# One scan over all 128 partitions for both directions of a state-space layer, the backward half turned round by ScalarE copies, with two sets of scan buffers

## The chip, the cores and the metric

The kernel is one program on one core of a Trainium2 chip. Its time is the device time of one execution in microseconds (us); the median of a few runs is compared. The core has a matrix engine (TensorE, PE in the profile; its weight loads are PEld), a vector engine (VectorE, DVE), a scalar engine (ScalarE, ACT), a general engine (GpSimd, POOL) and the queue that issues transfers (SyncE, SP). Each engine takes its instructions in a fixed order and starts one only when what it waits for is done; whatever stands behind a waiting instruction on that engine waits too.

## The reference

A bidirectional encoder block on x of 1 x 1024 x 1024 in float32. After an RMS norm and a projection, half of the channels go through state-space (S5) scans, the other half through a Fourier mix; then come an output projection and a gated feed-forward part with a short convolution. What the change touches is the scan:

```python
def s5_direction(uf, lam_re, lam_im, log_dt, b_re, b_im, c_re, c_im, reverse):
    ...
    bu = jnp.einsum('gph,blgh->blgp', b_bar, uf)
    a = jnp.broadcast_to(lam_bar, (1, uf.shape[1]) + lam_bar.shape)
    _, states = lax.associative_scan(_ssm_combine, (a, bu), reverse=reverse, axis=1)
    return jnp.einsum('ghp,blgp->blgh', c, states).real

y = s5_direction(..., False) + s5_direction(..., True)
```

There are 32 groups with 64 states each, once forward and once backward in time.

## The kernel before

The 1024 steps are laid as 128 chunks of 8 steps. Within a chunk the work is matrix products; only the state at the chunk borders needs a recurrence, a scan over 128 chunks. The complex factor of the recurrence is split into a modulus (`r8`, the factor of the real scan) and a phase that tables (`wt`) take out before the scan and put back after it.

The 32 groups are 16 batches of two (`NB = 16`, `NG = 2`). On the 128 partitions lie the 64 states of the forward direction (partitions 0 to 63) and the 64 of the backward direction (64 to 127). For each batch `states(b)` does, with the names that the profile shows:

- ACT fills `scr` with the scan's factor `r8`, spread over the chunks (line 740).
- DVE makes two products `r` of the chunk inputs `ps` (in PSUM) and the phase table (line 745); two sums of their halves go into `scd`, real and imaginary part (lines 747 and 749, each on DVE or POOL).
- DVE runs four scans: for the real and for the imaginary part, once partitions 0 to 63 forwards (line 756) and once partitions 64 to 127 read and written backwards (line 757). Two groups lie one behind the other in a row of 260 elements; columns of zeros between them restart the recurrence.
- Two products `x` of the scan's result `so` and the table (line 763) and two sums `yy` (line 764) put the phase back, each on DVE or POOL.

`outputs(b)` multiplies `yy` with the matrices `cm` on PE (tile `py`). Other functions run beside this: `prep` (`b`, `bt`, `bm`, lines 666 to 673), `tables` (`w`, `wt`, lines 710 to 714), `out_matrix` (`c`, `cm`, lines 721 to 725), the Fourier part (`vv`, `cb`, `pq`, `fw`, `yfs`, `yf`, lines 828 to 897) and the lower half of the output projection (`pwo`, `h`, line 931). The string `SEQ` gives the order in which these steps are recorded (`S:3` is `states(3)`), a table `ON` says for some 350 small operations whether DVE or POOL does them, and a scheduler then sets the order on each engine from its own estimate of times. So an edit of one step can move others. `scd`, `scr` and `so` exist once.

After the scans come the gate of the state-space half (line 990 on), the upper half of the output projection and the feed-forward part, where PE works nearly without a pause.

Of the kernel before, what the change touches and what calls it, by code (L numbers as in the profile page):

```python
# [15 lines left out]
AF = mybir.ActivationFunctionType  # L16
ALU = mybir.AluOpType
# [3 lines left out]
P = 128  # L21
# [3 lines left out]
NCH = 128  # L25
# [56 lines left out]
def bc(ap, axis, n):  # L82
    ap = ap.unsqueeze(axis)
    shape = list(ap.shape)
    shape[axis] = n
    return ap.broadcast_to(shape)
# [3 lines left out]
def encoder_block(  # L90
# [8 lines left out]
    V, A, PE, GP = nc.vector, nc.scalar, nc.tensor, nc.gpsimd  # L99
# [9 lines left out]
    def opt(key, default):  # L109
        v = OPT.get(key, default)  # L110
        return {"V": V, "G": GP}.get(v, v) if isinstance(v, str) else v
# [137 lines left out]
    def q(name, shape=(P, G), dt=F32, tag="q", bufs=13):  # L249
        return sp.tile(list(shape), dt, name=name, tag=tag, bufs=bufs)  # L250

    def keep(name, shape=(P, G), dt=F32):
        return sp.tile(list(shape), dt, name=name)

    NG = 2
    NB = G // NG
    W = 130

    xh = big.tile([P, 8, L], F32R, name="xh", tag="x32", bufs=2)
    xl = big.tile([P, 8, L], F32R, name="xl", tag="x32", bufs=2)  # L260
# [11 lines left out]
    def norm1(s):  # L272
        xr = xrs[s]
        ss = const.tile([P, 1], F32, name=f"n1_{s}_ss", tag="ss", bufs=2)
        junk = q(f"n1_{s}_sq", (P, 2 + 2 * NG * W), tag="so", bufs=1).bitcast(BF16)[:, 0:D]
        A.activation(junk, xr, AF.Square, accum_out=ss)
# [58 lines left out]
    r8 = keep("r8")  # L335
# [200 lines left out]
    dmk = keep("dmk", (P, 16))  # L536


    scd = keep("scd", (P, 2, NG, W))
    scr = keep("scr", (P, NG, W))  # L540
    cbr = keep("cbr", (P, 8, 2, 16))
    cbi = keep("cbi", (P, 8, 2, 16))

    def zeros():
        nc.sync.dma_start(dmk[96:128], dmask)
        for t in (scd, scr, cbr, cbi):
            GP.memset(t, 0.0)

    cw = const.tile([P, 188], F32, name="cw")
# [87 lines left out]
    def t2(name):  # L637
        return q(name, (P, 2 * NG * P), tag="t2", bufs=2)
# [97 lines left out]
    def states(b):  # L736

        c = bs[b]
        pst_ = c.ps
        A.activation(scr[:, :, 1:129], bc(r8[:, NG * b:NG * b + NG], 2, NCH), AF.Copy)  # L740
        sv = pst_.rearrange("p (i g c) -> p i g c", i=2, g=NG)
        wv = c.wt.rearrange("p i g j n -> p i g (j n)")
        for i in range(2):
            m = t2(f"r{b}_{i}").rearrange("p (i g c) -> p i g c", i=2, g=NG)
            V.tensor_mul(m, sv, wv if i == 0 else wv[:, ::-1])
            if i == 0:
                opt(f"ra{b}{i}", V).tensor_add(scd[:, 0, :, 1:129], m[:, 0], m[:, 1])
            else:
                opt(f"ra{b}{i}", V).tensor_sub(scd[:, 1, :, 1:129], m[:, 1], m[:, 0])
        n = 2 * NG * W  # L750
        so = q(f"so{b}", (P, 2 + n), tag="so", bufs=1)
        m = NG * W
        rf = scr.rearrange("p g w -> p (g w)")
        for i in range(2):
            df = scd[:, i].rearrange("p g w -> p (g w)")
            V.tensor_tensor_scan(so[0:64, 2 + i * m:2 + i * m + m], rf[0:64], df[0:64], 0.0, ALU.mult, ALU.add)
            V.tensor_tensor_scan(so[64:128, i * m:i * m + m][:, ::-1], rf[64:128, ::-1], df[64:128, ::-1], 0.0,
                                 ALU.mult, ALU.add)
        xs = so[:, 2:2 + n].rearrange("p (i g w) -> p i g w", i=2, g=NG)[:, :, :, :NCH]
        c.yy = q(f"yy{b}", (P, 2, NG, NCH), tag="yy", bufs=2)  # L760
        for i, op in ((0, ALU.subtract), (1, ALU.add)):
            m = t2(f"x{b}_{i}").rearrange("p (i g c) -> p i g c", i=2, g=NG)
            opt(f"xm{b}{i}", V).tensor_mul(m, xs, wv if i == 0 else wv[:, ::-1])
            opt(f"xa{b}{i}", V).tensor_tensor(c.yy[:, i], m[:, 0], m[:, 1], op)
# [176 lines left out]
    def w_out_bottom(n, s):  # L941
        w_out_rows(yf_k, wob[n], s, n)

    acts = {
        "N": norm1, "LW": load_win, "PR": params, "ME": zeros, "LG": load_g, "LX": load_x, "PO": poles, "PW": powers, "IF": input_factor,
        "PH": phasor, "PT": phase_tables, "GS": in_factors, "GO": out_factors, "RB": raw_b, "RC": raw_c,
        "CR": rows, "U": w_in_u, "LU": load_u, "P": prep, "T": tables, "OM": out_matrix, "I": inputs, "S": states,
        "O": outputs, "VI": w_in_v, "F": four_tables,
        "FA": four_fold, "FB": four_rows, "FC": four_cols, "ZS": zsplit, "HL": load_h, "WL": w_out_load,
# [432 lines left out]
    for i in range(2):  # L1382
        w = outer.tile([P, 2, 512], F32R, name=f"du{i}", tag="wp", bufs=NWP).bitcast(F32)
# [69 lines left out]
```

## Time and profile before

| | |
|---|---|
| median of 3 runs | 1065.32 us (1063.32 to 1065.96) |
| profiled execution, its own time | 1065.84 us |
| span in the profile | 1064.1 us |
| busy: PE / DVE / ACT / POOL | 91% / 88% / 44% / 22% |
| scans on DVE | 64, 55.0 us |
| mean granted TensorE clock | 0.972 of full speed |

The batches run from about 100 to 335 us after the span's start. How to read it: "busy" is the time in which an engine executes; the rest it waits, and the profile names what ended most of each wait. A time in a table of stretches is from the span's start. In a timeline the first number is the start, the second the duration, and the square bracket the wait before it.

### The profile page before, as it was taken

The numbers are of one execution on the slowest core, as the hardware profiler recorded it, in microseconds if no ns is written. First come the engines' busy times: TensorE is split into PE (matmuls) and PEld (weight loads), VectorE is DVE, ScalarE is ACT, GpSimd is POOL, SyncE is SP. The second block draws the span as 40 slices with busy tenths as digits, with TensorE's granted clock in tenths as the row PEclk, the third lists the DMA queues.
The fourth block names the chain that finished last, engine by engine and source line by source line (L and its number), as shares of the span: only waits on it lengthen the run. The fifth ranks groups of instructions, "written<-read, shape, count | busy, mean of one in ns | idle before, by whom it ended". The sixth has DMA issues, their size and how long they took to land.

```text
span 1064.1 us, 13493 instructions
## 1 busy us (share of the span) xinstructions
PE 969.6 (91%) x4504; PEld 798.9 (75%) x4504; DVE 939.0 (88%) x1721; ACT 465.5 (44%) x849; POOL 232.0 (22%) x243
## 2 busy tenths in 40 slices
PE   1798878677889999999999999999999999999996
PEld 1677767665767788788888888888887778888874
DVE  6998997999997899999988889888897678999887
ACT  4444222533122656544445444454453455445643
POOL 6247546775653003200000000000000000000400
PEclk9999998878999999999999999999999989999998
DMA  8262002342021323332322322223233399857544
GB/s 242 31 165 65 26 20 91 88 146 79 21 64 58 107 84 114 95 99 95 103 79 72 99 79 85 80 74 99 80 100 108 119 325 387 313 165 238 169 145 158
DMA packets 121595, 126.78 MB, mean 119 GB/s; under 512 B 17921, under 2 KB 86454, under 8 KB 121526
## 3 DMA queue, kind: packets, MB, share of 16 engines
q1 hardware_dynamic: 121382, 125.66, 37.2%
q8 instruction: 35, 0.57, 0.2%
q14 instruction: 34, 0.28, 0.1%
q10 hardware_dynamic: 144, 0.26, 0.1%
HBM read 103.35 MB, written 22.51 MB: 118 GB/s over the span
## 4 chain that ended last, share of the span: by engine, by line
PE 44%; DVE 9%; DMA 3%; issue 2%; ACT 1%; SPq 0%; DVEq 0%; ACTq 0%
PE u L130 33%; PE dqa L130 6%; PE dqb L130 6%; DMA wu<-in_w_up_dram 1%; DVE cg L1106 1%; DVE hb L1327 1%; DVE wo L155 0%; DMA d_3a<-adr 0%; ACT cg L1103 0%; DVE cv L1106 0%; DMA d_8a<-adr 0%; DVE n_t L196 0%; DMA d_7b<-in_w_down_dram 0%; DMA d_9b<-in_w_down_dram 0%; DVE hb L1311 0%
## 5 line engine op out<-in xcount | busy, mean ns | idle before, releaser
L1319 POOL TENSOR_TENSOR hb<-hb,gl 128x512 f32<-128x512 f32 x8 | 13.3, 1690 | 553.0 <-DMA d_9a<-adr 552.8
L130 PE MATMUL u<-xb,wo 128*128 128x512 f32 x528 | 130.0, 390 | 0.2 <-ACT xb L154 0.2
L130 PEld LDWEIGHTS u<-xb,wo 128*128 128x128 f32 x528 | 98.9, 188 | 21.8 <-ACT xb L154 0.6
L130 PE MATMUL u<-xa,wo 128*128 128x512 f32 x408 | 98.8, 390 | 0.6 <-DVE wo L155 0.5
L130 PEld LDWEIGHTS u<-xa,wo 128*128 128x128 f32 x408 | 76.4, 188 | 17.3 <-DVE wo L155 0.9
L154 ACT ACTIVATE wo<-wu 128x512 fp32r<-128x512 f32 x78 | 49.1, 630 | 86.5 <-PE u L130 58.7
L130 PE MATMUL pin<-xh,win 128*128 128x512 f32 x256 | 78.4, 407 | 1.2 <-ACT xh L227 1.2
L1106 DVE SCALAR_TENSOR_TENSOR cg<-ug,cw,cg 128x896 f32<-128x896 f32 (+1 forms) x88 | 62.5, 752 | 13.2 <-ACT cg L1103 13.2
L130 PE MATMUL u<-t4o,wo 128*128 128x512 f32 x264 | 63.4, 389 | 0.0
L1106 DVE SCALAR_TENSOR_TENSOR cv<-uv,cw,cv 128x896 f32<-128x896 f32 (+1 forms) x88 | 62.3, 752 | 0.0
L154 ACT ACTIVATE wo<-ws 128x512 fp32r<-128x512 f32 x32 | 20.2, 631 | 91.0 <-PE u L130 78.4
L130 PE MATMUL pwo<-wo,yf 128*128 128x512 f32 x192 | 49.9, 406 | 8.8 <-DVE h L931 5.3
L130 PEld LDWEIGHTS pin<-xh,win 128*128 128x128 f32 x256 | 49.1, 195 | 11.2 <-ACT xh L227 1.6
L130 PEld LDWEIGHTS u<-t4o,wo 128*128 128x128 f32 x264 | 49.6, 188 | 10.3
L155 DVE TENSOR_TENSOR wo<-wu,wo 128x512 fp32r<-128x512 f32 x78 | 55.1, 706 | 0.0
L130 PE MATMUL u<-t1o,wx 128*128 128x512 f32 x204 | 49.5, 389 | 0.0
L130 PE MATMUL u<-t2o,wx 128*128 128x512 f32 x204 | 49.5, 389 | 0.0
L130 PEld LDWEIGHTS pwo<-wo,yf 128*128 128x128 f32 x192 | 35.2, 192 | 17.4 <-DVE h L931 6.4
L130 PE MATMUL pin<-xl,win 128*128 128x512 f32 x128 | 46.4, 411 | 0.1
L130 PEld LDWEIGHTS u<-t2o,wx 128*128 128x128 f32 x204 | 38.3, 188 | 8.0
L130 PEld LDWEIGHTS u<-t1o,wx 128*128 128x128 f32 x204 | 38.3, 188 | 8.0
L714 ACT ACTIVATE wt<-wt 128x128 f32<-128x128 f32 x32 | 9.9, 309 | 67.8 <-POOL wt L712 44.1
(568 smaller groups left out, 2457.6 us busy)
## 6 DMA issues: line engine op xcount, KB each, us to landing
wu<-in_w_up_dram SPq DMA_DIRECT2D x88, 256.0 KB, 2.9
adr<-cg SPq DMA_DIRECT2D x22, 512.0 KB, 3.0
xr<-in_x_dram SPq DMA_DIRECT2D x8, 512.0 KB, 8.2
win_st<-in_w_in_dram SPq DMA_DIRECT2D x16, 256.0 KB, 2.9
wo_st<-in_w_out_dram SPq DMA_DIRECT2D x16, 256.0 KB, 2.8
h<-in_x_dram SPq DMA_DIRECT2D x8, 512.0 KB, 4.5
hdr<-h SPq DMA_DIRECT2D x8, 512.0 KB, 2.6
hb<-hdr SPq DMA_DIRECT2D x8, 512.0 KB, 6.3
```

The source lines that it names most:

```text
L130: i = PE.matmul(o, lhsT, rhs, start=start, stop=stop, skip_group_check=skip)
L154: A.activation(dst_hi, src, AF.Copy)
L155: return eng.tensor_sub(dst_lo, src, dst_hi.bitcast(F32))
L714: A.activation(wf[:, :, 0:64], wf[:, :, 127:63:-1], AF.Copy, scale=(-1.0 if i else 1.0))
L1106: V.scalar_tensor_tensor(cv[:, lo:hi], src[:, at:at + hi - lo], w, cv[:, lo:hi], ALU.mult, ALU.add)
L1319: GP.tensor_mul(hv(s, n), hv(s, n), gl[:, n * 512:(n + 1) * 512])
L1327: V.tensor_add(hv(s, n), hv(s, n), t)
```

## The change

A batch's chunk inputs for the backward direction are now laid in reversed order, so that one scan over 128 partitions goes forwards for both. The two sums go into a new tile `d` (named `sd`, two buffers). Two ACT copies bring `d` into `scd`: partitions 0 to 63 as they are, 64 to 127 with the chunks reversed (new lines 753 and 754). Then there are two scans instead of four (new line 757), and two more ACT copies bring `so` into a new tile `xs` (named `sx`, two buffers), the upper half reversed again (new lines 760 and 761). `scd` and `scr` now exist twice and are used in turn; a row of two groups is 258 elements instead of 260. Line numbers move by two from `states` on.

```diff
-    W = 130
+    W = 129
...
-    scd = keep("scd", (P, 2, NG, W))
-    scr = keep("scr", (P, NG, W))
+    scds = [keep(f"scd{i}", (P, 2, NG, W)) for i in range(2)]
+    scrs = [keep(f"scr{i}", (P, NG, W)) for i in range(2)]
...
-        for t in (scd, scr, cbr, cbi):
+        for t in (*scds, *scrs, cbr, cbi):
             GP.memset(t, 0.0)
...
-        A.activation(scr[:, :, 1:129], bc(r8[:, NG * b:NG * b + NG], 2, NCH), AF.Copy)
+        scr, scd = scrs[b % 2], scds[b % 2]
+        A.activation(scr[:, :, 1:W], bc(r8[:, NG * b:NG * b + NG], 2, NCH), AF.Copy)
...
+        d = q(f"sd{b}", (P, 2, NG, NCH), tag="sd", bufs=2)
...
-                opt(f"ra{b}{i}", V).tensor_add(scd[:, 0, :, 1:129], m[:, 0], m[:, 1])
+                opt(f"ra{b}{i}", V).tensor_add(d[:, 0], m[:, 0], m[:, 1])
...
+        A.activation(scd[0:64, :, :, 1:W], d[0:64], AF.Copy)
+        A.activation(scd[64:128, :, :, 1:W], d[64:128, :, :, ::-1], AF.Copy)
+        so = q(f"so{b}", (P, 2, NG, W), tag="so", bufs=1)
         for i in range(2):
-            df = scd[:, i].rearrange("p g w -> p (g w)")
-            V.tensor_tensor_scan(so[0:64, 2 + i * m:2 + i * m + m], rf[0:64], df[0:64], 0.0, ALU.mult, ALU.add)
-            V.tensor_tensor_scan(so[64:128, i * m:i * m + m][:, ::-1], rf[64:128, ::-1], df[64:128, ::-1], 0.0,
-                                 ALU.mult, ALU.add)
-        xs = so[:, 2:2 + n].rearrange("p (i g w) -> p i g w", i=2, g=NG)[:, :, :, :NCH]
+            V.tensor_tensor_scan(so[:, i].rearrange("p g w -> p (g w)"), scr.rearrange("p g w -> p (g w)"),
+                                 scd[:, i].rearrange("p g w -> p (g w)"), 0.0, ALU.mult, ALU.add)
+        xs = q(f"sx{b}", (P, 2, NG, NCH), tag="sx", bufs=2)
+        A.activation(xs[0:64], so[0:64, :, :, 0:NCH], AF.Copy)
+        A.activation(xs[64:128], so[64:128, :, :, NCH - 1::-1], AF.Copy)
```

The scheduler makes a new order of it. Where a scan stands it prints SCALAR_TENSOR_TENSOR; numbers behind a name only tell buffers apart. On DVE, batch 3 (the fourth) stood so before:

```order
L745 TENSOR_TENSOR r_0_1331<-ps_1263,wt_1116 128x512
L745 TENSOR_TENSOR r_1_1334<-ps_1263,wt_1116 128x512
L747 TENSOR_TENSOR scd<-r_0_1331 128x2x128
L749 TENSOR_TENSOR scd<-r_1_1334 128x2x128
L756 SCALAR_TENSOR_TENSOR so_1337<-scr,scd 64x260
L757 SCALAR_TENSOR_TENSOR so_1337<-scr,scd 64x260
L756 SCALAR_TENSOR_TENSOR so_1337<-scr,scd 64x260
L757 SCALAR_TENSOR_TENSOR so_1337<-scr,scd 64x260
L763 TENSOR_TENSOR x_0_1343<-so_1337,wt_1116 128x512
L763 TENSOR_TENSOR x_1_1346<-so_1337,wt_1116 128x512
```

and stands so now:

```order
L747 TENSOR_TENSOR r_0_1348<-ps_1275,wt_1124 128x512
L747 TENSOR_TENSOR r_1_1351<-ps_1275,wt_1124 128x512
L749 TENSOR_TENSOR sd_1347<-r_0_1348 128x256
L751 TENSOR_TENSOR sd_1347<-r_1_1351 128x256
L757 SCALAR_TENSOR_TENSOR so_1356<-scr_106,scd_104 128x258 x2
L765 TENSOR_TENSOR x_0_1363<-sx_1359,wt_1124 128x512
L765 TENSOR_TENSOR x_1_1366<-sx_1359,wt_1124 128x512
```

The ACT copies belong between the second `sd` and the scan, and between the scan and the first `x`; on DVE nothing stands at either place. In batch 5 the scheduler put other work there:

```order
L751 TENSOR_TENSOR sd_1735<-r_1_1739 128x256
L694 TENSOR_TENSOR dd_1612<-dd_1612,ds_1615 32x128
L695 TENSOR_TENSOR kf_991<-kf_991,dd_1612 32x128
L757 SCALAR_TENSOR_TENSOR so_1744<-scr_106,scd_104 128x258 x2
L693 TENSOR_TENSOR ds_2098<-ds_2098,dmk 32x128
L723 TENSOR_TENSOR cm_1460<-c_0_1461 128x256
L721 TENSOR_TENSOR c_1_1464<-pst,rawc 128x512
L725 TENSOR_TENSOR cm_1460<-c_1_1464 128x256
L765 TENSOR_TENSOR x_0_1751<-sx_1747,wt_1280 128x512
```

So two instructions stand ahead of the scan there and four behind it. On ACT, in batch 7, the two pairs of copies now stand with this between them:

```order
L753 ACTIVATE scd_104<-sd_1929 64x4x128
L754 ACTIVATE scd_104<-sd_1929 64x4x128
L814 ACTIVATE fw<-ft_1965 128x512
L814 ACTIVATE fw<-ft_1968 128x512
L780 ACTIVATE ys_1825<-py_1920 128x2x8x16
L673 ACTIVATE bm_1906<-pbm_1907 128x512
L814 ACTIVATE fw<-ft_1971 128x512
L680 ACTIVATE kf_1692<-pk_1913 128x32
L681 ACTIVATE kb_1693<-pk_1913 128x32
L760 ACTIVATE sx_1941<-so_1938 64x512
L761 ACTIVATE sx_1941<-so_1938 64x512
L741 ACTIVATE scr_106<-r_97 128x2x128
```

Before, the same seven instructions stood on ACT without copies around them. The fill of `scr` now follows the copies out of `so`.

## Rows read from the trace of the kernel before

**Rows 1.** Busy time of the engines in stretches of the span (us of each engine with the number of instructions, then the granted TensorE clock, the DMA share and GB/s): the stage of the scans as a whole, ten microseconds of it, its end, and a stretch after it.

```profile
100.00:330.00 230.00, 184.30 (x1005) 154.16 (x1004) 215.59 (x348) 69.22 (x188) 147.35 (x164) 0.90 0.21 62
...
310.00:320.00 10.00, 10.00 (x54) 8.59 (x53) 9.91 (x17) 1.20 (x4) 3.70 (x4) 1.00 0.28 83
...
300.00:345.00 45.00, 41.81 (x204) 34.14 (x203) 38.41 (x54) 12.72 (x27) 20.08 (x18) 0.96 0.19 55
...
500.00:600.00 100.00, 100.00 (x443) 82.57 (x442) 89.52 (x136) 46.43 (x65) 0.00 (x0) 1.00 0.29 90
```

**Rows 2.** Waits in that stage (who waits for whom: us in total, times, longest): of DVE the longest and the last of its eleven rows, with those on POOL, and the longest of all engines.

```profile
DVE bt L667 <- PE pk L130: 2.2, 1, 2.2
...
DVE r L745 <- POOL yy L764: 1.2, 2, 0.6
DVE cm L725 <- POOL c L721: 1.1, 1, 1.1
DVE w L710 <- POOL wt L712: 1.1, 1, 1.1
DVE cb L839 <- POOL vv L834: 1.0, 1, 1.0
DVE bt L667 <- POOL b L666: 1.0, 1, 1.0
...
DVE cb L844 <- POOL vv L835: 0.2, 1, 0.2
ACT scr L740 <- DVE so L757: 56.8, 14, 8.0
```

**Rows 3.** Groups of DVE instructions in the stage (busy us, mean ns of one, idle before them).

```profile
L756 DVE TENSOR_TENSOR_SCAN so<-scr,scd 64x260 f32<-64x260 f32 x32 | 28.0, 875 | 0.2
L757 DVE TENSOR_TENSOR_SCAN so<-scr,scd 64x260 f32<-64x260 f32 x32 | 27.0, 844 | 0.5
L745 DVE TENSOR_TENSOR r<-ps,wt 128x512 f32<-128x512 f32 x32 | 21.0, 679 | 1.4 <-POOL yy L764 1.2
L666 DVE TENSOR_TENSOR b<-gst,rawb 128x512 f32<-128x512 f32 x19 | 20.8, 1117 | 0.7 <-POOL yy L764 0.6
L763 DVE TENSOR_TENSOR x<-so,wt 128x512 f32<-128x512 f32 x22 | 19.3, 906 | 0.3
L667 DVE TENSOR_TENSOR bt<-b 128x256 f32<-128x256 f32 x22 | 15.8, 740 | 3.4 <-PE pk L130 2.2 <-POOL b L666 1.0
```

**Rows 4.** The first line of the scans alone: shortest, median and longest of its 32 instructions in ns, first and last start.

```profile
L756 DVE TENSOR_TENSOR_SCAN so<-scr,scd x32: 678/692/1591, 109.0 to 326.7; 64x260 f32<-64x260 f32 x32
```

**Rows 5.** Timeline of DVE: two instructions of the same kind, on 128 and on 32 partitions, and batch 3 from its second sum to the first product of the next batch.

```profile
101.97 0.29 DVE L712 TENSOR_TENSOR wt<-w 128x128 f32<-128x128 f32 x1
...
110.17 0.29 DVE L695 TENSOR_TENSOR kf<-kf,dd 32x128 f32<-32x128 f32 x1
...
140.00 0.41 DVE L749 TENSOR_TENSOR scd<-r 128x256 f32<-128x256 f32 x1
140.33 0.68 DVE L756 TENSOR_TENSOR_SCAN so<-scr,scd 64x260 f32<-64x260 f32 x1
...
142.45 0.70 DVE L757 TENSOR_TENSOR_SCAN so<-scr,scd 64x260 f32<-64x260 f32 x1
143.18 1.29 DVE L763 TENSOR_TENSOR x<-so,wt 128x512 f32<-128x512 f32 x2
```

**Rows 6.** Timeline of ACT: a fill of `scr` behind that scan, two copies of 512 elements in a row, and a copy that DVE waits for; the last line is the DVE instruction that it releases.

```profile
143.24 0.42 ACT L740 ACTIVATE scr<-r 128x256 f32<-128x256 f32 x1 [3.76 <-DVE so L757]
...
216.85 1.15 ACT L154 ACTIVATE yf<-yfs 128x512 fp32r<-128x512 f32 x2 [0.18 <-DVE yfs L893]
...
345.08 0.63 ACT L154 ACTIVATE wot<-wo_st 128x512 fp32r<-128x512 f32 x1 [2.37 <-DMA wo_st<-in_w_out_dram]
...
345.75 0.69 DVE L155 TENSOR_TENSOR wot<-wo_st,wot 128x512 fp32r<-128x512 f32 x1 [1.65 <-ACT wot L154]
```

**Rows 7.** Timeline of DVE: one each of the small instructions that the new order puts beside the scans.

```profile
179.21 0.41 DVE L725 TENSOR_TENSOR cm<-c 128x256 f32<-128x256 f32 x1
...
194.07 0.68 DVE L155 TENSOR_TENSOR fw<-pq,fw 128x512 fp32r<-128x512 f32 x1
...
277.33 0.69 DVE L931 TENSOR_TENSOR h<-h,pwo 128x512 f32<-128x512 f32 x1
```

**Rows 8.** Timeline of ACT around batch 7: three of the seven instructions that now stand between the pairs of copies.

```profile
195.68 0.38 ACT L778 ACTIVATE ys<-py 128x256 f32<-128x256 f32 x1 [1.01 <-PE py L130]
196.10 0.60 ACT L673 ACTIVATE bm<-pbm 128x512 f32<-128x512 f32 x1
196.60 0.62 ACT L812 ACTIVATE fw<-ft 128x512 fp32r<-128x512 f32 x1
```

**Rows 9.** The clearing of the scan buffers on POOL (line 547): shortest, median, longest in ns, first and last start.

```profile
L547 POOL MEMSET scd<- x1: 534/534/534, 1.0 to 1.0; 128x520 f32 x1
L547 POOL MEMSET scr<- x1: 314/314/314, 1.8 to 1.8; 128x260 f32 x1
```

More of the change, by code (lines that the diff above doesn't have):

```diff
@@ L746, in states @@
             if i == 0:
-                opt(f"ra{b}{i}", V).tensor_add(scd[:, 0, :, 1:129], m[:, 0], m[:, 1])
+                opt(f"ra{b}{i}", V).tensor_add(d[:, 0], m[:, 0], m[:, 1])
             else:
[L749 to L753, printed above, removed]
-        for i in range(2):
-            df = scd[:, i].rearrange("p g w -> p (g w)")
-            V.tensor_tensor_scan(so[0:64, 2 + i * m:2 + i * m + m], rf[0:64], df[0:64], 0.0, ALU.mult, ALU.add)
-            V.tensor_tensor_scan(so[64:128, i * m:i * m + m][:, ::-1], rf[64:128, ::-1], df[64:128, ::-1], 0.0,
-                                 ALU.mult, ALU.add)
-        xs = so[:, 2:2 + n].rearrange("p (i g w) -> p i g w", i=2, g=NG)[:, :, :, :NCH]
+                opt(f"ra{b}{i}", V).tensor_sub(d[:, 1], m[:, 1], m[:, 0])
+        A.activation(scd[0:64, :, :, 1:W], d[0:64], AF.Copy)
+        A.activation(scd[64:128, :, :, 1:W], d[64:128, :, :, ::-1], AF.Copy)
+        so = q(f"so{b}", (P, 2, NG, W), tag="so", bufs=1)
+        for i in range(2):
+            V.tensor_tensor_scan(so[:, i].rearrange("p g w -> p (g w)"), scr.rearrange("p g w -> p (g w)"),
[3 more added lines that the diff above has]
+        A.activation(xs[64:128], so[64:128, :, :, NCH - 1::-1], AF.Copy)
         c.yy = q(f"yy{b}", (P, 2, NG, NCH), tag="yy", bufs=2)
```

## The prediction

> **What bounds the kernel now.** First the busy times by stretch. While the batches run, from 100 to 330 us, DVE is busy 215.6 of 230 us, ACT 69.2 and POOL 147.4; PE reaches 184.3, at 0.90 of its full clock [rows 1]. DVE carries this stage. At its end PE takes over: it is busy in all of the ten microseconds from 310 on, and then for 100 of 100 us from 500 on [rows 1]. So what DVE gains or loses before about 306 us moves the end by as much; what the last three batches gain behind that is covered by PE. Next the waits: DVE has eleven, 11.6 us in all, the longest 2.2 us; eight of them, 6.8 us, are on POOL. The longest wait of the whole stage is ACT's for the scans, 56.8 us, and nothing on the path hangs on it [rows 2]. Then the groups: the 64 scans cost 28.0 + 27.0 = 55.0 us, a quarter of DVE's stage [rows 3].
>
> **What the change removes.** 64 scans over 64 partitions become 32 over 128, each 258 long instead of 260. Does a scan over twice the partitions take longer? No row has one. A two-input operation of 128 elements takes 0.29 us on 32 partitions and 0.29 on 128 [rows 5], so I take the same time. One scan costs 860 ns on average, though its median is 692 and its longest 1591 [rows 3, 4]. The products `r`, with one input in PSUM, never stretch: 679 ns for 512 elements, while `x` of the same size with both inputs in SBUF takes 906 and `b` 1117 [rows 3]. Something holds up what reads SBUF twice, and POOL is the engine that works beside it. At the mean the saving is 32 x 0.860 = 27.5 us; if only the undisturbed time goes it is 32 x 0.692 = 22.1; if a scan took twice as long it would be nothing. I take 27.5, since a scan that isn't there can't be held up, and keep 22.1 for the rivals.
>
> **What it adds.** Four copies of 512 elements per batch on ACT, 64 in all. The nearest rows are ACT copies of 512 elements on 128 partitions: two in a row take 1.15 us [rows 6]. 32 pairs are 36.8 us of ACT's time, which lifts it from 69 to 106 of 230 us; there is room. Bounds for a pair: 2 x 0.42 by the copy of 256 elements and 2 x 0.63 by two that don't overlap [rows 6]. The price lies in the order. A DVE instruction that used the result of the one ahead of it now waits for ACT. From DVE to ACT: the last scan ends at 142.45 + 0.70 = 143.15, ACT starts at 143.24, so 0.09. From ACT to DVE: 345.08 + 0.63 = 345.71, DVE starts at 345.75, so 0.04 [rows 5, 6]. One hand-over is 0.09 + 1.15 + 0.04 = 1.28 us, two per batch. All 32 uncovered would be 41.0 us, more than the saving. Behind the waiting scan stands everything else on DVE, and POOL and PE wait for that.
>
> How many are covered? I went through the new order batch by batch and set the DVE instructions between sum and scan, and between scan and `x`, against 1.28 us, at their short durations of 0.41 for `cm` and 0.68 for `fw` or `h` [rows 7]. Batch 3 has nothing at either place, as the order in the section on the change shows: 2.56 us of standing, against 3.4 saved at the mean and 1.4 at the median. Batch 5 covers both almost wholly. Ahead of the scans, batches 0 to 15 leave 1.3, 1.0, 0.9, 1.3, 0.9, 0.1, 1.3, 1.3, 0, 1.3, 0.9, 0, 0.9, 0.6, 0, 0.6, together 12.4 us. Behind them they leave 0.6, 1.3, 0.9, 1.3, 1.3, 0, 1.3, 1.3, 0, 1.3, 0, 1.3, 1.3, 0, 0 and 1.3, together 13.2, and I add 0.9 for POOL's `x` in batch 13. That is 26.5 us, as if 20.7 of the 32 were bare.
>
> Four smaller terms. ACT takes its instructions in order: in batch 7 seven of them now stand between the two pairs of copies, some 2.5 us from start to start (0.4 to 0.5 each for the larger ones [rows 8]), while the two scans take 1.4, so 1.1 more; batch 0 gives 0.6. With as much again for places that I didn't see, +3 us. In return DVE's busy share falls from 94% to 82%. The stretching of scans, `x`, `b` and `bt` beyond their short times (0.69, 0.68, 0.68, 0.41) is about 31 us in the rows, 26 of it left when half the scans are gone, and falls by about an eighth: -3.3 us. While DVE stands, POOL catches up on part of the 6.8 us: -2. Batches 13 to 15 save 5.2 and stand 2.5, and this 2.7 stays under PE: +2.7.
>
> At nothing I put the rest. ACT no longer waits with the fill of `scr` alone, but the copies out of `so` wait for the same scan, so little behind it starts earlier. Two more buffers are cleared on POOL: 0.53 + 0.31 us in the first three microseconds [rows 9], long before the first scan. If that cover went it would be 0.85.
>
> Sum against the profiled execution's own 1065.84 us: -27.5 + 26.5 + 3 - 3.3 - 2 + 2.7 = -0.6, so 1065.2. That execution lies 0.5 above the median of the runs, which gives 1064.7.
>
> The Trainium skill speaks against the copies. "ScalarE: Activation LUTs", section "Rules for kernel authors", budgets about 0.3 us for an ACTIVATE and 0.83 ns for each element. An estimate by that page is 0.72 us for a copy and 1.45 for a pair, 0.3 more at each of 20.7 bare hand-overs, so 6 us more and 1071. The pair of 1.15 us that was measured decides [rows 6].
>
> **The rivals.** *Better covered.* ACT is idle most of the time, so its queue may cost nothing (-3); DVE standing still may end all of POOL's waits (-4.8 more) and halve the stretching again (-3.3): 11 us less, 1053. For it speaks that DVE's waits on POOL are short ones; against it that these relieve only where POOL is behind at that moment.
>
> *Slower: ACT's queue.* The mechanism is one: a copy stands behind one more ACT instruction that isn't done. An ACT instruction takes 69.2 / 188 = 0.37 us on average [rows 1]; at 20.7 bare hand-overs that is 7.7 us, so 1072. It decides as soon as more than 27.5 / 1.28 = 21.5 hand-overs' worth of waiting is bare, and I count 20.7. Batch 7 speaks for it; ACT's low share against it.
>
> *Slower: the hold-ups are passed on.* If POOL holds whatever DVE instruction comes, a scan that is gone hands its hold-up to the next. Then only 22.1 us are saved, 5.4 less: 1070. For it speaks that scans with a median of 692 reach 1591. Against it, DVE stands still more often and POOL passes in those gaps. The Trainium skill's page "SBUF — State Buffer", section "Who interferes with whom", says that a DVE instruction with two SBUF inputs and a GpSimd instruction that reads SBUF contend and that one blocks; `r` at 679 ns with no stretching agrees.
>
> *It doesn't do what it says*, a scan over 128 partitions taking twice as long: 1092. The rows of 0.29 us speak against it; I give it nothing of its own.
>
> **How the numbers follow.** What a measurement of this kernel can tell from no change is about 0.3%, 3.2 us. The forecast, that gain and standing cancel, 1064.7, has 0.40 and its own range is 1060 to 1069; 0.09 of it lies faster, 0.27 within the bound and 0.04 slower. Better covered has 0.31, ACT's queue 0.21, the passed-on hold-ups 0.08. So faster 0.09 + 0.31 = 0.40, same 0.27, slower 0.04 + 0.21 + 0.08 = 0.33. The range reaches past the rival on either side, 1050 to 1078; all hand-overs bare (14.5 us more than now, 1079) or all covered (1038) stay outside.
>
> **What will show it.** 32 scans at 0.69 to 0.9 us each; pairs of copies at 1.15; DVE waiting on ACT for `scd` and `sx` about 26 us in all, near 2.5 in batch 3 and near none in batch 5; DVE busy about 30 us less over the stage, and the gate of the state-space half starting within 4 us of where it did. I am wrong if DVE's waits for those copies come to under 18 or over 35 us, if the other two-input operations keep their mean times, or if PE's granted clock in the stage moves by more than a few hundredths of its 0.90.

## The result and the profile after

The changed kernel takes 1067.82 us (median of nine runs, 1066.13 to 1069.73), the kernel before in the same session 1064.51 (1062.23 to 1066.75). The ratio is 1.0031, with a 95% interval of 1.0018 to 1.0044: slower by 3.3 us, between 1.9 and 4.7. The forecast was 1064.7 us, "that gain and standing cancel". The time lies inside the forecast's range. "Slower" by more than 0.3% had a chance of 0.33; the measured 0.31% sits on that bound, and its interval excludes only that nothing changed.

The profiled execution of the changed kernel lies low among its nine: its own time is 1066.17 us, its span 1064.4, against 1065.84 and 1064.1 before, where it lies high. So the two traces explain 0.3 us of the 3.3 directly; they show what the operations cost, and the ratios of repeated runs show what that is worth.

Busy time by stretch in the changed kernel, with the columns of [rows 1]:

```profile
100.00:330.00 230.00, 179.19 (x1002) 151.88 (x1001) 182.13 (x313) 107.76 (x248) 145.38 (x163) 0.89 0.21 62
...
500.00:600.00 100.00, 100.00 (x442) 82.61 (x441) 89.46 (x137) 46.52 (x65) 0.00 (x0) 1.00 0.28 88
```

The prediction expects DVE busy about 30 us less; it is 33.5 less (215.59 in [rows 1]) and ACT 38.5 more. PE's clock is 0.89 instead of 0.90. From 500 to 600 us nothing has changed. The same stretch reaches 230 us all the same, so DVE now stands for 33.5 us more. Whom it waits for, from 100 us to the start of the gate of the state-space half at 347.2 us (who waits for whom: us in total, times, longest):

```profile
DVE x L765 <- ACT sx L761: 14.6, 12, 2.5
DVE so L757 <- ACT scd L754: 10.8, 10, 1.4
DVE sg L993 <- issue: 4.2, 1, 4.2
DVE bt L667 <- POOL cm L725: 3.5, 1, 3.5
DVE yy L766 <- POOL x L765: 3.4, 2, 2.2
DVE cm L725 <- POOL c L721: 2.7, 2, 1.7
DVE r L747 <- ACT wt L714: 2.6, 1, 2.6
DVE b L666 <- POOL yy L766: 1.9, 1, 1.9
DVE r L747 <- POOL yy L766: 1.7, 3, 0.6
...
DVE w L710 <- POOL wt L712: 1.0, 1, 1.0
...
DVE a L847 <- POOL vv L837: 0.8, 1, 0.8
...
DVE c L721 <- POOL cm L723: 0.6, 1, 0.6
...
```

The first two rows are the hand-overs: 25.4 us at 22 of 32 places, 10.8 ahead of the scans and 14.6 behind them. Among the rows under them is what the prediction missed: DVE's waits on POOL, eight rows, are 15.6 us by these names; before they were 6.8 [rows 2]. One of the eight is PE's. `bt` doesn't read `cm`; it exists once, PE's `pk` of the batch before reads it, and it starts 0.10 us after the last of these ends (167.69 + 0.39 = 168.08):

```profile
167.69 0.39 PE L130 MATMUL pk<-cbi,bt 128*128 128x32 f32 x2
...
168.18 0.99 DVE L667 TENSOR_TENSOR bt<-b 128x256 f32<-128x256 f32 x1 [3.55 <-POOL cm L725]
```

It waited for `pk` before too (2.2 us). Without it DVE's waits on POOL are 12.1 us.

The groups that answer to [rows 3] (busy us, mean ns of one, idle before them):

```profile
L757 DVE TENSOR_TENSOR_SCAN so<-scr,scd 128x258 f32<-128x258 f32 x32 | 24.9, 818 | 10.8 <-ACT scd L754 10.8
L747 DVE TENSOR_TENSOR r<-ps,wt 128x512 f32<-128x512 f32 x32 | 21.3, 682 | 4.7 <-ACT wt L714 2.6 <-POOL yy L766 1.7
L666 DVE TENSOR_TENSOR b<-gst,rawb 128x512 f32<-128x512 f32 x19 | 19.1, 1023 | 2.0 <-POOL yy L766 1.9
L765 DVE TENSOR_TENSOR x<-sx,wt 128x512 f32<-128x512 f32 x22 | 15.0, 711 | 14.6 <-ACT sx L761 14.6
L667 DVE TENSOR_TENSOR bt<-b 128x256 f32<-128x256 f32 x22 | 13.5, 631 | 3.5 <-POOL cm L725 3.5
```

A scan over 128 partitions takes what one over 64 took. 55.0 us of scans have become 24.9, and `x`, `b` and `bt` are held up less. Batch 3 on DVE, as in [rows 5]:

```profile
140.90 0.41 DVE L751 TENSOR_TENSOR sd<-r 128x256 f32<-128x256 f32 x1
142.66 1.28 DVE L757 TENSOR_TENSOR_SCAN so<-scr,scd 128x258 f32<-128x258 f32 x2 [1.35 <-ACT scd L754]
145.28 1.29 DVE L765 TENSOR_TENSOR x<-sx,wt 128x512 f32<-128x512 f32 x2 [1.33 <-ACT sx L761]
147.19 0.69 DVE L747 TENSOR_TENSOR r<-ps,wt 128x512 f32<-128x512 f32 x1 [0.62 <-POOL yy L766]
```

and on ACT:

```profile
141.35 0.63 ACT L753 ACTIVATE scd<-sd 64x512 f32<-64x512 f32 x1 [2.60 <-DVE sd L751]
142.00 0.63 ACT L754 ACTIVATE scd<-sd 64x512 f32<-64x512 f32 x1
143.98 0.63 ACT L760 ACTIVATE sx<-so 64x512 f32<-64x512 f32 x1 [1.35 <-DVE so L757]
144.62 0.63 ACT L761 ACTIVATE sx<-so 64x512 f32<-64x512 f32 x1
```

Both hand-overs are bare here, 1.35 and 1.33 us. The two copies of a pair don't overlap: 141.35 to 142.63 is 1.28 us, about the upper of the prediction's two bounds (2 x 0.63), not the 1.15 that it took from [rows 6]. The next batch's `r` starts at 147.19, where it started at 145.09 before. In batch 7 the wait behind the scans is 2.48 us, as the prediction feared, with seven instructions on ACT between the pairs:

```profile
202.03 0.69 DVE L765 TENSOR_TENSOR x<-sx,wt 128x512 f32<-128x512 f32 x1 [2.48 <-ACT sx L761]
```

### The profile page after: what moved, and what is told of

It reads as the page before. It is cut to its first block, busy times and chain, and to the rows that moved or that the text cites. A ratio compares the mean times of both kernels' runs of the same rounds, so it can differ in the third digit from the quotient of the medians.

```text
span 1064.4 us, 13516 instructions
## 1 busy us (share of the span) xinstructions
PE 965.3 (91%) x4504; PEld 796.5 (75%) x4504; DVE 906.1 (85%) x1689; ACT 505.0 (47%) x913; POOL 231.1 (22%) x245
## 4 chain that ended last, share of the span: by engine, by line
PE 50%; DVE 5%; DMA 2%; issue 1%; ACT 1%; DVEq 0%; ACTq 0%
PE u L130 34%; PE dqa L130 9%; PE dqb L130 7%; DMA wu<-in_w_up_dram 1%; DVE cg L1108 1%; DVE wo L155 0%; DMA d_7b<-in_w_down_dram 0%; DVE n_t L196 0%; ACT cg L1105 0%; DMA first_st<-in_w_down_dram 0%; DVE hb L1313 0%; DMA d_9b<-in_w_down_dram 0%; DMA d_5b<-in_w_down_dram 0%; DMA d_3b<-in_w_down_dram 0%; DVE n_y L197 0%
## 5 line engine op out<-in xcount | busy, mean ns | idle before, releaser
L130 PEld LDWEIGHTS u<-xa,wo 128*128 128x128 f32 x408 | 76.4, 188 | 17.6 <-DVE wo L155 1.1
L221 PE MATMUL n_pt<-ident,xr 128*128 128x128 f32 x64 | 13.2, 358 | 26.3 <-DVE xr L292 9.6
```

Source lines behind the costliest of these rows:

```text
L130: i = PE.matmul(o, lhsT, rhs, start=start, stop=stop, skip_group_check=skip)
L221: PE.transpose(pt[:, k * P:(k + 1) * P], xk, ident)
```

## The experiments

The theories, as the expectations name them. *Hand-over*: DVE pays for standing between two of its own instructions while ACT copies, and for what comes of it. *Order*: the scheduler has made a new order, and its waits are that order's, whatever runs in it. *PE*: PE limits the stage, so DVE's gain is hidden anyway. A percentage below is the ratio to the kernel before in the same session; 1% is 10.65 us.

### Buffers, and the copies one place at a time

The first four kernels were left to the scheduler. The kernel before with two sets of buffers:

```diff
-    scd = keep("scd", (P, 2, NG, W))
+    scds = [keep(f"scd{i}", (P, 2, NG, W)) for i in range(2)]
...
+        scr, scd = scrs[b % 2], scds[b % 2]
```

> The kernel before with scd and scr twofold and nothing else: still four scans per batch, no copies. If the slowdown comes from the hand-overs to ACT and what follows from them, the buffers alone are worth nothing: 1064 to 1066 us, and DVE's waits in the batches stay near 12 us. If it comes from the new order that the scheduler makes as soon as anything in the stage changes, this kernel too moves by 2 us or more, with DVE's waits on POOL grown as in the changed kernel.

Measured: 1063.55 us, ratio 1.0001 (0.9988 to 1.0014). The buffers are worth nothing, and by themselves they move nothing.

The changed kernel without copies, and with those at one of the two places:

```diff
-        d = q(f"sd{b}", (P, 2, NG, NCH), tag="sd", bufs=2)
+        d = scd[:, :, :, 1:W]
...
-        A.activation(scd[0:64, :, :, 1:W], d[0:64], AF.Copy)
-        A.activation(scd[64:128, :, :, 1:W], d[64:128, :, :, ::-1], AF.Copy)
...
-        A.activation(xs[0:64], so[0:64, :, :, 0:NCH], AF.Copy)
-        A.activation(xs[64:128], so[64:128, :, :, NCH - 1::-1], AF.Copy)
+        xs = so[:, :, :, 0:NCH]
```

> The changed kernel without any ACT copy: the sums go straight into scd and x reads so, so 32 scans of 128 partitions remain. It leaves out the turning round of the backward half. Theory hand-over: DVE loses 33.5 us of busy time and the 25.4 us of waits for copies don't come, and with them the other waits (23 us in the changed kernel) fall back to about 12, as before; the gate starts some 30 us earlier, 1036 us. Rival order: the other waits stay near 23 us because they belong to the new order, 1046 us. Rival PE: what DVE gains is mostly hidden because PE becomes the bound of the stage, 1055 us or more.

> The changed kernel with the copies ahead of the scan alone; x reads so directly. It leaves out the second turning, so the upper half of the result is in the wrong order. Theory hand-over: 10.8 us of waits for these copies and half of the 11 us of other waits, 16 us over the kernel without copies: 1052 us. Rival order: the waits for scd cost their 10.8 us alone, and the other waits are what the order gives, near 23 us: 1057 us. Rival PE: no more than 3 us from the kernel without copies.

> The changed kernel with the copies behind the scan alone; the sums go straight into scd. It leaves out the first turning. Theory hand-over: 14.6 us of waits for sx and half of the 11 us of other waits, 20 us over the kernel without copies: 1056 us, and the excess of this one and of the one with the copies ahead add up to that of the changed kernel over the kernel without copies. Rival order: 14.6 us alone, other waits near 23: 1060 us, and the two don't add up. Rival PE: no more than 3 us from the kernel without copies.

Measured: 1058.44 us without copies (0.9953, 0.9936 to 0.9970), 1050.43 with those ahead of the scan (0.9890, 0.9872 to 0.9908), 1056.01 with those behind it (0.9948, 0.9930 to 0.9966). The first was expected at 1036 us by *hand-over*, 1046 by *order* and 1055 or more by *PE*, so by itself it would speak for *PE*. But the kernel without any copy is the slowest of the three, so nothing adds up. Each has its own order, and what the orders differ by hides the copies. No theory is told apart by kernels that the scheduler arranges anew.

### The order held

So the order was made a quantity of its own. From the finished order of one kernel, a list per engine says which instruction follows which; each is made to follow the one before it in another kernel too:

```diff
+        for a, b in zip(names, names[1:]):
+            tc.add_manual_dep(
+                here["I-" + b], "I-" + a,
+                mybir.DependencyInfo(mybir.DependencyClass.NoSync, mybir.DependencyReason.DATA),
+                reason="issue order",
+            )
```

Of DVE, POOL, ACT and PE all instructions are held, from the input matrices of the first batch to the sums or outputs of the last. Copies that the order's own kernel doesn't have, or has otherwise, find their place freely.

> The changed kernel, with the instructions of DVE, POOL, ACT and PE between the first batch's tables and the last batch's sums held in the order that the kernel before has; the four copies of a batch go where the scheduler finds room. In that order hardly anything stands between sum, scan and x, so more hand-overs are bare: 28 to 32 of them at 1.28 us, 36 to 41 us of waits for copies, against 33.5 us of DVE time saved. Theory order: the other waits of DVE fall from 23 us to the 12 us of the kernel before, so 1065 to 1072 us. Theory hand-over: they stay at 20 us or more, because POOL and PE are late with what comes from a DVE that stands, 1075 us or more.

> The kernel before with twofold buffers, four scans and no copies, with the instructions of the four engines held in the order of the changed kernel. Theory order: the 11 us of other waits came with that order, so this kernel shows them too, about 23 us in all, and takes 1070 us or more. Theory hand-over: the order costs nothing by itself, DVE's waits stay near 12 us and the time at 1063 to 1066 us.

> One scan over 128 partitions and no copies, in the order of the kernel before: the scan saving alone. It leaves out the turning round of the backward half. Theory order: the 33 us of DVE time come off the stage nearly in full, because no other order spoils them: 1033 to 1042 us, where the same kernel in the scheduler's own order took 1058. Rival PE: TensorE with its lower clock becomes what DVE and POOL wait for, and no more than 10 us come off: 1053 us or more.

> One scan over 128 partitions and no copies, in the order of the changed kernel; it leaves out the turning round of the backward half. With it each of the three sets of operations has run in that order or can be set against it: four scans took 1066, one scan with copies 1068. In the order of the kernel before, the copies cost 32 us (1078 against 1047). Theory hand-over (the 25 us of waits for copies are paid in full): 1043 us. Rival cover (of what DVE gains, only about half reaches the end, as 33 us became 18 in the order of before, so the copies in the order that was made for them cost half of their waits): 1053 to 1057 us. Theory order (the order is bad for whatever runs in it): 1060 us or more.

Measured, with the runs of the kernels before and after in the table:

| | order of before | order of after |
|---|---|---|
| four scans, no copies | 1.0000 | 1.0011 (1.0000 to 1.0021) |
| one scan, no copies | 0.9832 (0.9817 to 0.9847) | 0.9850 (0.9830 to 0.9870) |
| one scan, four copies | 1.0127 (1.0107 to 1.0148) | 1.0031 (1.0018 to 1.0044) |

This takes the 3.3 us apart. The new order alone costs 0.11%, 1.2 us (0 to 2.2). In it the scans save 1.61%, 17 us. In it the copies cost 1.81%, 19 us; by the intervals either is known to some 2 us. What is left of two large terms is 2 us, and the order's 1.2 comes on top. The trace doesn't locate the 1.2: with four scans in the new order the gate starts at 346.0 us, 1.0 earlier than before. In the order of before the scans save 1.68% and the copies cost 2.95%, 31 us: the new order is the scheduler's work to cover them. There DVE waits 36.0 us for copies:

```profile
DVE so L757 <- ACT scd L754: 20.8, 15, 2.9
DVE x L765 <- ACT sx L761: 15.2, 11, 2.1
```

The same two rows of the changed kernel, above, are 10.6 us less, most of it ahead of the scans.

Without copies, in the order of after, the stretch up to the gate is this (busy times as in [rows 1]):

```profile
100.00:324.70 224.70, 190.15 (x1086) 163.28 (x1085) 195.13 (x327) 76.81 (x198) 149.41 (x165) 0.92 0.23 69
```

and with them:

```profile
100.00:347.20 247.20, 195.85 (x1083) 165.47 (x1082) 192.09 (x327) 116.24 (x262) 149.22 (x166) 0.90 0.21 63
```

DVE is idle for 224.70 - 195.13 = 29.6 us in the one and 55.1 in the other. The difference, 25.5, is as much as the 25.4 us of waits for copies; DVE's busy time is 3.0 less with the copies, and the gate starts 22.5 us later. So *hand-over* holds in kind, but not in full: it gave 1043 us without copies in the order of after, *cover* 1053 to 1057, and 1049.62 came. In the order of before 1046.63 came, between the 1033 to 1042 of *order* and the 1053 of *PE*. With the copies there, 1078.38 is in *hand-over*'s range (1075 or more), while DVE's other waits ahead of the gate, 17.6 us, lie between what either theory gave. *PE* falls as the limit: PE gave way by 22 us as soon as DVE didn't stand. Of *order* its first half is right and its second wrong. Four scans in the new order do show DVE's waits ahead of the gate's grown, from 14.3 to 20.0 us:

```profile
DVE bt L667 <- PE pk L130: 3.3, 1, 3.3
DVE cm L725 <- POOL c L721: 2.7, 2, 1.7
DVE r L746 <- ACT wt L714: 2.6, 1, 2.6
DVE b L666 <- POOL yy L765: 1.8, 1, 1.8
DVE r L746 <- POOL yy L765: 1.7, 3, 0.6
...
```

but 1070 us or more were expected and 1066.3 came: DVE is also held up less in that order, and its busy time up to the gate is 7.0 us less than before. (*Hand-over* gave 1063 to 1066, with waits near 12.) The product `x` there, with four scans and no copies:

```profile
L764 DVE TENSOR_TENSOR x<-so,wt 128x512 f32<-128x512 f32 x22 | 14.8, 700 | 0.3
```

It took 906 ns in [rows 3]. With one scan and no copies, in the same order, it is back:

```profile
L761 DVE TENSOR_TENSOR x<-so,wt 128x512 f32<-128x512 f32 x22 | 19.2, 899 | 0.3
```

So neither a standing DVE nor ACT's copies are needed for 700 ns. What runs on POOL beside it matters: in the traces of before, of after, and of the order of after without copies with four scans and with one, 134 scans and `x` on DVE have no POOL instruction beside them, and none of them takes over 699 ns; of the 146 that have one, 79 take over 760. Running beside POOL isn't enough, though, and which POOL instructions do it wasn't separated.

All four copies in the order of the kernel that has only those ahead of the scan:

> The changed kernel with all its copies, in the order of the kernel that has the copies ahead of the scan alone (the fastest so far, 1050 us). Theory order: of the 14 us between that one and the changed kernel a part is the order, the second pair of copies adds at most 16 bare hand-overs of 1.28 us, 20 us; since that order leaves room for few of them, 1060 to 1070 us. Theory hand-over: the pair behind the scan costs its waits of 15 us and as much again in waits elsewhere, 1072 us or more.

Measured: 1079.63 us, 1.0139 (1.0124 to 1.0154). The time is in *hand-over*'s range (1072 or more). Of 31.1 us of waits for copies 18.7 are behind the scan, where the kernel of that order has none, and DVE's other idle time up to the gate grew by 10 us, not by as much again as expected.

### How long a copy may take

With the order of after held, one copy over 128 partitions at each place, which turns nothing:

```diff
-        A.activation(scd[0:64, :, :, 1:W], d[0:64], AF.Copy)
-        A.activation(scd[64:128, :, :, 1:W], d[64:128, :, :, ::-1], AF.Copy)
+        A.activation(scd[:, :, :, 1:W], d, AF.Copy)
```

> The changed kernel, in its own order on every engine, with one ACT copy over 128 partitions at each of the two places instead of two over 64; it leaves out the turning round of the backward half. A hand-over is then 0.09 + 0.63 + 0.04 = 0.76 us instead of 1.28. Theory hand-over (what is paid is the standing time): of 25.4 us of waits for copies some 10 to 11 go; taking both pairs away brought 18 us for 25, so these bring 7 to 8: 1060 us. Rival crossing (what is paid is that DVE has to go through ACT's queue at all, whatever the copy takes): 2 us or less, 1066 us or more.

Measured: 1055.55 us, 0.9914 (0.9892 to 0.9936). Its waits for copies:

```profile
DVE x L763 <- ACT sx L759: 7.5, 10, 1.9
DVE so L756 <- ACT scd L753: 4.5, 7, 0.8
```

12.0 us instead of 25.4, and the time is 1.17% less, 12.5 us, where *hand-over* expected 7 to 8. So the time follows the waits, by about 0.9 us for each of these; taking away the other 12.0 brought another 0.64%, 7 us, 0.6 for each. The rival, that the crossing as such costs (1066 us or more), falls.

Then a version that leaves nothing out: the copies split by real and imaginary part, so that the first two run beside the second sum or scan.

```diff
+            A.activation(scd[0:64, i, :, 1:W], d[0:64, i], AF.Copy)
+            A.activation(scd[64:128, i, :, 1:W], d[64:128, i, :, ::-1], AF.Copy)
```

> The changed kernel with each pair of copies of 512 elements split into two pairs of 256, one for the real and one for the imaginary part: the first pair can run while the second sum (or the second scan) does. Theory hand-over: the wait ahead of x falls from 1.28 to about 0.8 us and the wait ahead of the first scan to about 0.6, so of 25 us of waits some 12 go, and half of that reaches the end: 1062 us. Rival ACT queue: 64 more instructions on ACT, 14 us more, and four places instead of two where a copy can stand behind other work: 1068 us or more.

> The copies split by real and imaginary part, as in the kernel that took 1063.7 us, with the other instructions in the order of the changed kernel. Theory hand-over: the shorter wait is what helped, so it helps here too: waits for copies near 18 us instead of 25, 1062 to 1064 us. Rival order: the 4 us came from another order, and here the time stays at 1067 us or more.

Measured: 1063.68 us in its own order (0.9981, 0.9966 to 0.9996) and 1063.04 in the order of after (0.9985, 0.9968 to 1.0001). The second is in *hand-over*'s range (1062 to 1064), the first 2 us above its 1062. With the order held that is 0.46% less than the changed kernel, 5 us, for 17.4 us of waits for copies instead of 25.4. Part of the 8 us came back: DVE's waits on ACT apart from these copies went from 6.1 to 11.0 us, with 64 more instructions in ACT's queue.

### Other ways to turn the backward half

Each sum in two halves of 64 partitions, the upper one written in reversed order, without copies:

```diff
+            for hs, to in ((LO, scd[LO, i, :, 1:W]), (HI, scd[HI, i, :, NCH:0:-1])):
```

> The same result as the changed kernel without its ACT copies: each sum is made in two halves of 64 partitions, the upper one written in reversed chunk order. 39 more sums of 0.34 us from start to start on DVE, 13 us, against 33 us less for scans and stretching, and no hand-over; 25 more of about 0.5 us on POOL. DVE's balance is 20 us. Theory hand-over: without waits for ACT the balance counts, and as 33 us became 18 at the end, 20 become 11: 1053 us. Rival order: the scheduler's own order spoils it as it did for the kernel without copies (1058 where the order of before gave 1047): 1063 us or more.

Measured: 1074.07 us, 1.0085 (1.0068 to 1.0102), slower than both and a miss. Up to the gate DVE is busy 228.5 us, where without copies, in the order of after, it is 195.1. Of these 33.4 us the sums take 27.9 (52.9 for 78 against 25.0 for 39), 0.72 for each one more and not 0.34; the rest lies in other instructions of another order. A sum over 64 partitions isn't cheaper, and it reads SBUF twice:

```profile
L752 DVE TENSOR_TENSOR scd<-r 64x256 f32<-64x256 f32 x26 | 15.5, 594 | 0.3
```

The inputs turned by PE, which reads the chunks backwards for the upper 64 columns of weights:

```diff
+                for hs, st in ((LO, 1), (HI, -1)):
+                    c.s_last = PE.matmul(pst_[hs, n * P:(n + 1) * P], c.bm[:, i, g, hs],
+                                         cts[ct].u[:, NG * sb + g, ::st], start=True, stop=True)
```

> The same result with the inputs turned by PE: per batch eight products with 64 columns of weights in place of four with 128, the upper four reading the chunks in reversed order; the table of phases for the upper half takes the other sign, and only the sums yy are made in halves. DVE's balance is 33 - 17 x 0.34 = 27 us; PE gets 64 products of 0.3 us more, 19 us. Theory hand-over: DVE decides, half of 27 us reaches the end: 1050 us. Rival PE: the stage is as much PE's as DVE's, and 19 us of PE's time eat the gain: 1062 us or more.

> The kernel whose inputs PE turns (1058.8 us in the scheduler's own order), with the instructions of the four engines in the order of the kernel before. The kernel without copies took 1047 in that order and 1058 in its own. Theory order: this one gains as much, less what 17 more sums on DVE cost: 1050 to 1054 us. Rival PE: 64 more products on PE are the limit in any order: 1058 us or more.

> The same kernel in the order of the changed kernel, where the one without copies took 1050 us. Theory order: 1052 to 1056 us. Rival PE: 1058 us or more.

Measured: 1058.81 us in its own order (0.9944, 0.9926 to 0.9962), 1067.35 in that of before (1.0023, 1.0009 to 1.0037), 1060.26 in that of after (0.9960, 0.9946 to 0.9975). Faster than both kernels, but no more than half of what was expected, and in the order of before not at all. By the times alone the rival *PE* (1058 us or more, 1062 in the kernel's own order) would have it in both held orders. The traces speak against it. The sixteen half products of a batch run in pairs, two starting some 10 ns apart, and take no longer than the eight whole ones did, so the 19 us of PE's time that the expectation counted didn't come. Before, and with the halves (from the last but one kernel of this section, which turns the inputs in the same way):

```profile
105.29 1.14 PE L733 MATMUL ps<-u,bm 128*128 128x128 f32 x8
...
137.96 1.09 PE L734 MATMUL ps<-u,bm 128*64 128x128 f32 x16
```

What costs is on DVE. The 34 halved sums `yy` take 25 to 27 us, 786 ns on average in the kernel's own order, where 17 whole ones took 13.4. DVE is busy 216.3 us up to the gate in the order of before and 208.0 in that of after, and the gate starts 8.1 us later; the sums differ by 1.1 us of it, the scans by 3.5 and `b` by 3.2. Why they are held up more in one order isn't settled.

Last, the copies moved to where no DVE instruction waits for them: PE turns the inputs, and the sums `yy` are turned by ACT on their way to PE.

```diff
+            opt(f"xa{b}{i}", V).tensor_tensor(yy[:, i], m[:, 0], m[:, 1], op)
+            A.activation(c.yy[0:64, i], yy[0:64, i], AF.Copy)
+            A.activation(c.yy[64:128, i], yy[64:128, i, :, ::-1], AF.Copy)
```

> The same result with no copy between two instructions of DVE: PE turns the inputs, and the upper half is turned back by ACT copies of the sums yy, which go on to PE alone. No half sums, so DVE does what it does in the kernels without copies (1047 to 1058 us in three orders); PE has 64 products more, and its last products of a batch start some 1 us later. Theory hand-over: a copy costs where DVE waits for it, so this one costs next to nothing, 1048 to 1056 us. Rival PE: 1058 us or more.

Measured: 1055.83 us, 0.9902 (0.9882 to 0.9921): 10 us faster than the kernel before, 14 faster than the change, the fastest of those that leave nothing out, and at the upper end of what *hand-over* gave (1048 to 1056). ACT copies for 26 us here:

```profile
L765 ACT ACTIVATE yz<-yy 64x256 f32<-64x256 f32 x32 | 13.2, 415 | 25.7 <-DVE yy L764 18.6 <-POOL yy L764 4.1 <-DVE cb L846 2.9
L766 ACT ACTIVATE yz<-yy 64x256 f32<-64x256 f32 x32 | 13.1, 413 | 0.4
```

and none of DVE's waits up to the gate is for one of these copies, in a list that begins

```profile
DVE h L933 <- PE pwo L130: 7.6, 5, 2.0
DVE cm L723 <- POOL c L721: 5.5, 1, 5.5
DVE wot L155 <- ACT wot L154: 3.8, 1, 3.8
...
```

What the copies cost here beyond DVE's waits isn't separated: this kernel has its own order, and without copies 1047, 1050 and 1058 us were measured in three.

The same with the inputs turned by ACT on their way out of PSUM:

```diff
+        A.activation(sv[0:64], pv[0:64], AF.Copy)
+        A.activation(sv[64:128], pv[64:128, :, :, ::-1], AF.Copy)
```

> As the kernel that turns behind the sums, but the inputs are turned by two ACT copies that take them out of PSUM, not by PE. DVE waits for ACT once per batch at most, ahead of the first product, which other work can fill; PE has nothing more to do; the 32 products r now read SBUF twice and can be held up by POOL, 0.2 us each as x was, 7 us. Theory hand-over: 1052 to 1060 us. Rival held up: what r loses eats what PE gains, 1060 us or more.

Measured: 1061.70 us, 0.9966 (0.9952 to 0.9980). DVE waits 1.0 us for these copies, so again their place is cheap, but `r` now reads SBUF twice:

```profile
L750 DVE TENSOR_TENSOR r<-pz,wt 128x512 f32<-128x512 f32 x32 | 29.2, 936 | 2.6 <-ACT pz L745 1.0 <-POOL yy L766 0.6 <-ACT wt L714 0.5
```

936 ns for what took 682 from PSUM: 8 us, as the rival had it.

## Why the prediction came out on the wrong side

**The scans: right.** "32 scans at 0.69 to 0.9 us each" are 818 ns on average. The scans' own time fell by 30.1 us instead of 27.5. (The 3.4 us that the prediction sets against batch 3's standing is 1.7, since two scans of a batch go and not four; its sum doesn't use it.)

**The hand-overs: right.** 26.5 us were worked out place by place and 25.4 measured, 10.8 + 14.6 for 12.4 + 14.1. One costs 1.35 us and not 1.28, as the copies of a pair don't overlap; 25.4 us are 19.8 hand-overs of the prediction's 1.28, for 20.7. Batch 5 was covered almost wholly, as forecast (0.26 us ahead of its scan, none ahead of `x`).

**ACT's queue: half right.** Batch 7's wait is there, but it lies inside the 25.4. The +3 for it came in elsewhere, as waits for ACT other than these copies: 2.5 us before, 6.1 after.

**The stretching: right in size, not in its reason.** Beyond the scans DVE's busy time fell by 34.1 - 30.1 = 4.0 us up to the gate (226.2 before, 192.1 after), for 3.3. But four scans in the new order, with DVE standing 6 us more than before and not 34, lose 7.0 us of busy time, so the order does it without a standing DVE. The one scan then gives part of it back (`x` from 700 to 899 ns), and the copies, with the order held, take off 3.0 us in the order of after and 7.2 in that of before. The reason given, DVE's lower share, is one part of three.

**POOL catches up: this step failed.** "While DVE stands, POOL catches up on part of the 6.8 us: -2." DVE's waits on POOL rose from 6.8 to 12.1 us, so the term is +5.3. The kernels with the order of after share it out: 9.2 with four scans (2.4 from the order), then, apart from the `bt` above, 10.7 with one scan and no copies, 11.5 with one copy at a place and 12.1 with two. (That `bt` waits for `pk` in all of these but the one without copies, where POOL's `b` ends its 2.9 us.) In the order of before they rise from 6.8 to 10.9 without copies. So a standing DVE doesn't shorten these waits, and most of the rise comes without its standing. POOL is busy about 150 us in each. That a DVE that needs less time comes sooner to what POOL makes is the likely reason, argued and not shown; so is a second one, that some of POOL's work, `x` and `yy` above all, waits for DVE and ACT itself. The terms up to the gate are now -34.1 us of busy time, +25.4 for the copies, +3.6 for ACT otherwise, +5.3 for POOL and nothing for the rest of the idle time, together +0.2: the gate starts at 347.2 us where it started at 347.0. The prediction has -3.3 for the same terms; POOL is 7.3 off, and the others make up 3.8 of it. No run separates the +2.7 for the last three batches.

**One for one: not so.** "What DVE gains or loses before about 306 us moves the end by as much." DVE's busy time (third number of those with a count) in the stretch up to the gate, before, with four scans in the order of after, and with one scan and no copies in the order of before:

```profile
100.00:347.00 247.00, 201.08 (x1090) 168.16 (x1088) 226.21 (x361) 77.06 (x201) 150.88 (x166) 0.91 0.22 65
...
100.00:346.00 246.00, 197.53 (x1080) 170.07 (x1079) 219.18 (x359) 77.41 (x198) 150.75 (x165) 0.88 0.21 63
...
100.00:331.90 231.90, 198.50 (x1090) 167.01 (x1088) 201.32 (x329) 76.60 (x202) 148.27 (x166) 0.91 0.23 69
```

In the order of after, one scan instead of four takes 24.1 us off DVE's busy time (219.2 to 195.1), 21.3 off the gate and 17 off the end; 25.4 us of waits cost 22.5 at the gate and 19 at the end. The ends are those of the repeated runs. The profiled executions from which the gates are taken end 21.0 and 19.6 us apart (1067.63 and 1066.17 against 1046.58). In the order of before, 24.9 us off DVE became 15.1 at the gate, as DVE's idle time rose from 20.8 to 30.6. Of the 30.8 us forecast for scans and stretching 17 reached the end, of the 29.5 for the hand-overs and ACT's queue 19. Both errors are large and nearly cancel, and that the forecast is no more than 3 us off is luck to this extent; what they leave is that the copies cost 2 us more than the scans save.

**What no term had** is the order as such, 1.2 us. With it the three parts of the table make +0.31%, by construction; what the table adds is their sizes.

**The rivals.** *Better covered* was wrong: DVE's waits on POOL rose instead of ending, and those on ACT apart from the copies rose too. *ACT's queue*, 1072 us, was to decide from 21.5 bare hand-overs; by the same measure there were 19.8. *The hold-ups are passed on* is half true where DVE doesn't stand: with the order held and no copies DVE's busy time falls by 24.9 us in the order of before and 24.1 in that of after, between the rival's 22.1 and the 27.5. In the order of before the 32 scans themselves take 932 ns on average and save 26.4; in that of after they take 817, and other instructions take up the hold-ups, `x` above all. *It doesn't do what it says* is out. In the Trainium skill, "SBUF — State Buffer", section "Who interferes with whom", the reason given is that DVE's second SBUF input and GpSimd's reads share one interface and exclude each other; `r` at 682 ns from PSUM and 936 from SBUF agrees.

Not located in a trace: of the 3.3 us, the 3.0 that these two profiled executions don't differ by.

## What to carry to other kernels

A copy on another engine between two dependent instructions of the bound engine holds that engine for its whole length plus the two crossings, here 1.33 to 1.35 us, wherever the order has nothing to put there, and of 25.4 us of such waits 19 reached the end. Moved to an edge that leaves the bound engine for good, copies of 26 us were waited for by no DVE instruction, and that kernel was the fastest whole one. When a bound engine gets faster, count the waits on the engine beside it as growing, not as shrinking: here they grew from 6.8 to 10.9 us in the order of before, with POOL's work unchanged. And before two scheduled kernels are compared term by term, hold the order: here the same work without copies took 1047, 1050 and 1058 us in three orders.

## What the runs showed of the hardware

A scan of 258 elements over 128 partitions has a median of 696 ns, one of 260 over 64 a median of 692 [rows 4]: the second 64 partitions cost nothing here. The converse surprised more. A sum of 256 elements over 64 partitions takes 594 to 865 ns on average where both inputs lie in SBUF beside a busy POOL, one over 128 takes 501 to 796 without copies in the order of after, so halving by partitions about doubled the cost of the sums (25.0 to 52.9 us). On PE it was the other way: 16 products with 64 columns of weights each, in pairs for the two halves of the partitions, take 1.09 us, 8 with 128 columns 1.14. And two ACT copies of 64 x 512 that follow each other on the same tiles take 1.28 us from the first start to the last end, with no overlap, where two of 128 x 512 took 1.15 [rows 6]; one over 128 partitions takes the same 0.63 us as one over 64.
